# A decoder trunk's last down projection: square sums and products of its tails by halves, residual sums of seven tiles on ScalarE and GpSimd, Newton steps of five tiles on GpSimd

## The chip, the core and the metric

The kernel runs on one core of a Trainium2 chip. The time is device microseconds of one execution. Engines are named as the profile has them: PE (matmul), DVE (vector), ACT (scalar), POOL (GpSimd) and SP, whose queue issues most DMAs.

## The reference

One inference step of a hybrid decoder of two layers, in float32: 1024 prompt tokens and 64 sample tokens, model width 1024, feed-forward width 2816. Layer 0 is a state-space mixer and a convolutional feed-forward block, layer 1 differential attention over a shared cache and another feed-forward block. The change lies in the last lines of layer 1:

```python
def rmsnorm(x, g):
    y = xf * lax.rsqrt(jnp.mean(xf * xf, axis=-1, keepdims=True) + NORM_EPS)
    return (y * g.astype(jnp.float32)).astype(x.dtype)
...
    out = (jax.nn.gelu(gate) * val) @ w_down
...
        f_out, buf = conv_ffn(rmsnorm(x, p['f_pre_g'][i]), conv_buf0[i], p['w_up'][i], p['conv_w'][i],
                              p['conv_b'][i], p['w_down'][i])
        x = x + rmsnorm(f_out, p['f_post_g'][i])
```

So the down projection's output of a token (1024 values) needs the sum of its squares, a reciprocal root, the product with a gain row, and the sum with the residual x; for layer 1 that is the output y.

## The kernel before

Tokens lie on the 128 partitions: eight prompt tiles of 128 tokens (numbered 0 to 7) and one sample tile of 64 (number `NTT` = 8). A tile's result is a 128x1024 accumulator in SBUF, `acc[tt]`.

`ffn_down` works through the 2816 rows of the weight in chunks. In the last layer the last chunk has four blocks of 128 rows and goes by pairs of tiles: first the sample tile, then pairs (0,1), (2,3), (4,5), (6,7) (`LORD`). A pair is one level of a Strassen-Winograd scheme over two tiles and two 512-column halves: seven products (`b11`, `t1`, `t2`, `b21`, `b22`, `t3`, `t4`), each two times three float32 matmuls of 128x512 (each operand is a high and a low part), into PSUM. After each, `add` (L1426 to L1428) has DVE add a PSUM bank to one half of an accumulator: `acc<-mm,acc`, 128x512. Operand sums for the scheme are made by POOL from `gr` (loaded from DRAM scratch `gd`, L1355; sums L1360 to L1363) and split into high and low parts by ACT (L144) and DVE (L145).

`pair` is a generator. The loop over steps runs its seven parts with j = 0 to 6, and at j = 2 does three things: `flush` runs the last part of the pair before, `dn.upto` loads for the next pair, and `finish` calls `done` for the tiles in `ends`. In the last pair of the last layer (`norm` is False) `finish` is not called there; it is called after the loop.

`done` calls `tail_a`: a square sum of the whole tile on ACT (L824, with an accumulator read of 0.19 us), the product with the gain row on DVE (L851), `rstd_from` (L111 on: two small DVE instructions L120 and L123, then three Newton steps of two instructions each, L130 and L134, on one element a partition; with `aside` the steps go to POOL, L126 and L127), the residual sum in one DVE instruction (L854: acc times the root plus x) and the output's DMA on SP's queue (L855). Tile 7 does product, sum and output in two halves. After each tail, `fetch` (L1383) issues the load of the residual x for a tile three or four further on, `xr<-x3d` or `raw<-x3d`.

`part`, used elsewhere in the kernel, is the form of the tail's beginning by a piece: a square sum of a slice, one small DVE instruction (L838, or L835 for a second piece) and the product of the slice (L839). `rstd_from` then takes the partial value as `pre` and uses L122 in place of L120.

The order of the instructions on each engine is fixed when the kernel is built: a scheduler lays the operations out by its own estimates of their times and of what each waits for. On the chip each engine runs its queue in that order.

Of the kernel before, what the change touches and what calls it, by code (L numbers as in the profile page):

```python
# [15 lines left out]
ALU = mybir.AluOpType  # L16
# [5 lines left out]
D = 1024  # L22
# [6 lines left out]
NTT = SEQ // P  # L29
# [44 lines left out]
def trunk_kernel(ctx, tc, I, O):  # L74
    nc = tc.nc
    V = nc.vector
    A = nc.scalar
    PE = nc.tensor
    GP = nc.gpsimd
# [733 lines left out]
    def tokens(tt):  # L813
        return (tt * P, P) if tt < NTT else (SEQ, TS)
# [6 lines left out]
    def square_sum(y, n):  # L821
        junk = slot("junk", dtype=BF16)
        ss = slot("ss")
        A.activation(junk[0:n, 0 : y.shape[1]], y, AF.Square, accum_out=ss[0:n])  # L824
        return ss[0:n]
# [3 lines left out]
    def part(y, tt, post, cs):  # L829

        n = tokens(tt)[1]
        ss = square_sum(y, n)
        if tt in sums:
            p = sums[tt]
            V.scalar_tensor_tensor(p, ss, -0.5 / D, p, op0=ALU.mult, op1=ALU.add)  # L835
        else:
            p = sums[tt] = pools["ph"].tile([P, 1], F32, tag=f"pre{tt}", name=nm("pre"), bufs=1)[0:n]
            V.tensor_scalar(p, ss, -0.5 / D, -0.5 * EPS, op0=ALU.mult, op1=ALU.add)  # L838
        V.tensor_tensor(y, y, post[0:n, cs], ALU.mult)  # L839

    def tail_a(y, tt, post, xsrc, xdst, last=False, rest=slice(0, D), aside=False, xr=None):


        t0, n = tokens(tt)
        if xr is None:
            xr = slot("xr")
            nc.sync.dma_start(xr[0:n], xsrc(tt))
        halves = (slice(512, D), slice(0, 512)) if last else (slice(0, D),)
        ss = square_sum(y[:, rest], n)
        for hs in halves if last else (rest,):  # L850
            V.tensor_tensor(y[:, hs], y[:, hs], post[0:n, hs], ALU.mult)  # L851
        r = rstd_from(pools["ph"], ss, 1, n, "n1", bufs=4, pre=sums.pop(tt, None), aside=aside)
        for hs in halves:
            V.scalar_tensor_tensor(y[:, hs], y[:, hs], r[0:n], xr[0:n, hs], op0=ALU.mult, op1=ALU.add)  # L854
            nc.sync.dma_start(xdst(tt)[:, hs], y[:, hs])  # L855

    def tail_n(y, tt, aside, gain=None):
# [515 lines left out]
    def ffn_down(dn, i, xsrc, xdst, norm):  # L1373
        acc, res = {}, {}
        post = [None]
        nch = len(dn.plan)

        def fetch(j):

            if not norm and j <= NTT:  # L1380
                tt = ORDER[j]
                r = slot("xr") if j % 2 else pools["w"].tile([P, 1024], F32, tag="raw", name=nm("raw"), bufs=2)
                nc.sync.dma_start(r[0 : tokens(tt)[1]], xsrc(tt))  # L1383
                res[tt] = r

        def done(tt):
            n = tokens(tt)[1]
            y = acc[tt][0:n, 0:D]
            if n < P:
                for h in range(2):  # L1390
                    hs = slice(512 * h, 512 * h + 512)
                    u = slot("gr")
                    A.copy(u[0:n], acc[tt][n : 2 * n, hs])
                    V.tensor_tensor(y[:, hs], y[:, hs], u[0:n], ALU.add)
            if norm:
                tail.add(y, tt, post[0], xsrc, xdst)
            else:
                tail_a(y, tt, post[0], xsrc, xdst, tt == NTT - 1, xr=res.pop(tt))
                fetch(ORDER.index(tt) + 4)

        def plain(k, c, tt):
            kind, f0, nf = dn.plan[c]
            n = tokens(tt)[1]
            if c == 0:
                acc[tt] = slot("acc")
            gx, ws = dn.gx.pop(k), dn.ws[c]
            pa = [psum(), psum()]
            for f in range(nf):
                wh, wl = ws[f]
                st, sp = f == 0, f == nf - 1  # L1410
                if n == P:
                    seq = ((gx[:, f, 0:P], wh), (gx[:, f, 0:P], wl), (gx[:, f, P : 2 * P], wh))
                else:
                    seq = ((gx[:, f, 0 : 2 * n], wh), (gx[:, f, 0 : 2 * n], wl))
                for j, (lt, wt) in enumerate(seq):
                    for h in range(2):
                        PE.matmul(pa[h], lt, wt[:, h * 512 : (h + 1) * 512],  # L1417
                                  start=st and j == 0, stop=sp and j == len(seq) - 1)
            for h in range(2):
                a = acc[tt][:, h * 512 : (h + 1) * 512]  # L1420
                if c == 0:
                    A.copy(a, pa[h])
                else:
                    V.tensor_tensor(a, pa[h], a, ALU.add)

        def add(tt, h, ps):  # L1426
            a = acc[tt][:, h * 512 : (h + 1) * 512]
            V.tensor_tensor(a, ps, a, ALU.add)  # L1428

        def sample(k, c):  # L1430
            gx, ws = dn.gx.pop(k), dn.ws[c]

            def prod(ps, o, w, start):
                for e in range(2):
                    for j in range(2):
                        PE.matmul(ps, gx[:, 2 * e + o, 0 : 2 * TS], ws[e, w][j], start=start and e + j == 0,  # L1436
                                  stop=e + j == 2, skip_group_check=True)

            p1, p2 = psum(), psum()
            prod(p1, 0, "b11", True)  # L1440
            add(NTT, 1, p1)
            prod(p2, 0, "t1", True)
            prod(p2, 1, "b22", False)
            add(NTT, 1, p2)
            prod(p1, 1, "b21", False)
            add(NTT, 0, p1)

        def pair(k, c, ta):

            gx, ws = dn.gx.pop(k), dn.ws[c]  # L1450

            def prod(ps, w, start):
                for e in range(2):
                    (ah, al), (wh, wl) = gx[e], ws[e, w]
                    o = dn.AOP[w]
                    mm3(ps, ah[:, o], al[:, o], wh, wl, start and e == 0, e == 1, True)

            p1, p2 = psum(), psum()
            prod(p1, "b11", True)
            add(ta, 0, p1)  # L1460
            yield
            prod(p2, "t1", True)
            add(ta + 1, 1, p2)
            yield
            yield
            prod(p1, "t2", False)
            add(ta, 1, p1)
            yield
            p3 = psum()
            prod(p3, "b21", True)  # L1470
            add(ta, 0, p3)
            yield
            prod(p2, "b22", False)
            add(ta, 1, p2)
            yield
            prod(p1, "t3", False)
            add(ta + 1, 1, p1)
            yield
            prod(p1, "t4", False)
            add(ta + 1, 0, p1)  # L1480
            yield

        rest, ends = [], []

        def flush():

            while rest:
                g, cn = rest.pop()
                next(g)
                dn.load(cn, 1)  # L1490

        def finish():
            while ends:
                done(ends.pop(0))

        for k, (c, tt) in enumerate(dn.steps):
            kind, f0, nf = dn.plan[c]
            if c == nch - 1 and post[0] is None:
                post[0] = row_bcast(I["f_post_g"][i])
                for j in range(4):  # L1500
                    fetch(j)
            if kind == "p":
                dn.upto(k + 2)
                plain(k, c, tt)
                flush()
                if c == 0:
                    dn.load(1, 2)
            elif tt == NTT:
                sample(k, c)
                flush()  # L1510
                dn.upto(k + 1)
                finish()
            else:
                last = tt == 6
                g = pair(k, c, tt)
                for j in range(7):
                    if j == 2:
                        flush()
                        dn.upto(k + 1)
                        if not (norm is False and last):  # L1520
                            finish()
                    next(g)
                    if last and j != 2:
                        dn.load(c + 1, 1)
                if not last:
                    dn.load(c + 1, 1 if norm and c == nch - 2 else (3, 2, 2)[tt // 2])
                rest.append((g, c + 1 if last else nch))
            if c == nch - 1:
                ends += [tt] if kind == "p" or tt == NTT else [tt, tt + 1]
                if kind == "p":  # L1530
                    finish()
        flush()
        finish()
        tail.norm()
# [569 lines left out]
```

## Time and profile before

| | us |
|---|---|
| median of three runs | 2679.99 (2677.94 to 2682.68) |
| the profiled execution | 2684.83 |
| its span, first to last instruction | 2682.9 |
| TensorE clock granted, mean of the span | 0.976 |
| PE, DVE, ACT, POOL busy over the span | 2500.6, 1963.5, 1270.9, 657.3 |
| first residual sum of the stage (sample tile, L854) | from 2638.46 |
| last transfer's issue to the span's end | 2679.02 to 2682.9 |

The profile was taken in an execution of its own, so its span is set against 2684.83 and not against the median. Times in its timeline count from the span's start. The stage that the change touches is the last 60 us. A row of the timeline is start, duration, engine, line, operation, output tile, input tiles, and in brackets the idle time ahead of it with what ended it. DVE's instructions overlap a little: an instruction's duration is some 0.06 to 0.08 us more than the distance to the next start.

### The profile page before, as it was taken

How to read it: one execution, taken by the hardware profiler on the slowest of the kernel's cores; microseconds unless marked ns; L12 is line 12 of the kernel's file. 1: busy time of each engine (PE TensorE's matmuls, PEld its weight loads, DVE VectorE, ACT ScalarE, POOL GpSimd, SP SyncE). 2: the span in 40 equal slices, each digit the busy share in tenths (PEclk: the TensorE clock that was granted, in tenths of full speed). 3: DMA queues.
4: the chain of work that ended last, by engine and by line, in shares of the span. 5: the costliest groups of instructions: out<-in, count | busy, mean ns of one | idle time of the engine just before them, and what ended most of it. 6: DMA issues, size and time to landing. Idle time of an engine off the chain costs nothing.

```text
span 2682.9 us, 39622 instructions
## 1 busy us (share of the span) xinstructions
PE 2500.6 (93%) x14234; PEld 2203.5 (82%) x14234; DVE 1963.5 (73%) x3683; ACT 1270.9 (47%) x2559; POOL 657.3 (24%) x1062
## 2 busy tenths in 40 slices
PE   3778998999999989999999899989799999998997
PEld 2777887999999967778777788877699999996775
DVE  7994358777777789984232688875877777778999
ACT  6763334444444454354322677764544444444432
POOL 3220030111111175501201222113011111137661
PEclk9999998999999999999999899999899999999998
DMA  5443233222222233444646433335322222233334
GB/s 145 99 98 88 85 124 124 65 83 74 74 74 74 89 116 92 127 145 166 204 157 211 104 79 95 97 105 171 115 69 79 74 74 74 74 104 107 94 102 145
DMA packets 265688, 286.77 MB, mean 107 GB/s; under 512 B 42268, under 2 KB 212564, under 8 KB 265492
## 3 DMA queue, kind: packets, MB, share of 16 engines
q1 hardware_dynamic: 261892, 273.55, 33.0%
q0 software_dynamic: 3088, 9.77, 1.7%
q8 instruction: 113, 1.85, 0.3%
q10 hardware_dynamic: 512, 0.92, 0.1%
q14 instruction: 83, 0.68, 0.1%
HBM read 193.58 MB, written 70.93 MB: 99 GB/s over the span
## 4 chain that ended last, share of the span: by engine, by line
PE 58%; DVE 13%; DMA 4%; issue 3%; ACT 3%; POOL 2%; SPq 0%; DVEq 0%; POOLq 0%; ACTq 0%
PE mm L809 17%; PE mm L810 17%; PE mm L811 17%; DVE acc L1428 2%; DMA gr<-gd 1%; DVE xT_lo L145 1%; DVE S L1898 1%; PE mm L1417 1%; ACT S L1902 1%; DVE wst L145 1%; DVE xT_hi L145 1%; DVE acc L854 1%; PE mm L1436 1%; PE tr L870 1%; PE mm L1926 1%
## 5 line engine op out<-in xcount | busy, mean ns | idle before, releaser
L809 PE MATMUL mm<-xT_hi,whi 128*128 128x384 f32 (+1 forms) x1408 | 457.0, 325 | 2.0 <-ACT acc L1146 1.8
L810 PE MATMUL mm<-xT_lo,whi 128*128 128x384 f32 (+1 forms) x1408 | 456.3, 324 | 1.6 <-DVE xT_lo L145 1.6
L811 PE MATMUL mm<-xT_hi,wlo 128*128 128x384 f32 (+1 forms) x1408 | 454.2, 324 | 0.0
L809 PEld LDWEIGHTS mm<-xT_hi,whi 128*128 128x128 f32 x1408 | 265.4, 189 | 3.8 <-ACT acc L1146 2.4
L810 PEld LDWEIGHTS mm<-xT_lo,whi 128*128 128x128 f32 x1408 | 265.7, 189 | 2.4 <-DVE xT_lo L145 2.3
L811 PEld LDWEIGHTS mm<-xT_hi,wlo 128*128 128x128 f32 x1408 | 265.4, 189 | 0.8
L1195 POOL COPY cvo<-acc 128x2 f32<-128x2 f32 x88 | 53.3, 606 | 818.5 <-ACT acc L1178 818.5
L809 PE MATMUL mm<-whi,xT_hi 128*128 128x512 f32 x608 | 243.9, 404 | 4.9 <-ACT whi L792 4.7
L1192 DVE SCALAR_TENSOR_TENSOR acc<-acc,cpar,acc 128x1104 f32<-128x1104 f32 x176 | 240.0, 1385 | 4.7 <-ACT acc L1190 4.6
L810 PE MATMUL mm<-wlo,xT_hi 128*128 128x512 f32 x608 | 241.9, 398 | 0.1
L811 PE MATMUL mm<-whi,xT_lo 128*128 128x512 f32 x608 | 241.7, 399 | 0.0
L144 ACT CAST whi<-raw 128x1024 fp32r<-128x1024 f32 x88 | 92.5, 1051 | 253.5 <-PE mm L811 245.2
L1428 DVE TENSOR_TENSOR acc<-mm,acc 128x512 f32<-128x512 f32 x279 | 184.7, 680 | 9.8 <-PE mm L811 9.3
L145 DVE TENSOR_TENSOR wlo<-raw,whi 128x1024 fp32r<-128x1024 f32 x88 | 107.7, 1224 | 107.0 <-PE mm L810 91.6
L809 PE MATMUL mm<-acc,whi 128*128 128x384 f32 x528 | 179.1, 339 | 0.0
L811 PE MATMUL mm<-acc,wlo 128*128 128x384 f32 x528 | 178.7, 339 | 0.0
L810 PE MATMUL mm<-acc,whi 128*128 128x384 f32 x528 | 178.3, 338 | 0.0
L809 PEld LDWEIGHTS mm<-whi,xT_hi 128*128 128x128 f32 x608 | 115.6, 191 | 36.2 <-ACT whi L792 5.6
L810 PEld LDWEIGHTS mm<-wlo,xT_hi 128*128 128x128 f32 x608 | 114.7, 189 | 27.8 <-DVE wlo L793 0.8
L811 PEld LDWEIGHTS mm<-whi,xT_lo 128*128 128x128 f32 x608 | 114.4, 188 | 27.6 <-issue 0.8
L1190 ACT ACTIVATE acc<-acc,cpar 128x1104 f32<-128x1104 f32 x88 | 114.1, 1311 | 18.1 <-DVE acc L1161 11.9
L145 DVE TENSOR_TENSOR wlo<-xr,whi 128x1024 fp32r<-128x1024 f32 x88 | 107.6, 1223 | 16.7 <-ACT whi L144 8.6
(572 smaller groups left out, 6255.9 us busy)
## 6 DMA issues: line engine op xcount, KB each, us to landing
raw<-in_w_up_dram SPq DMA_DIRECT2D x88, 512.0 KB
gd<-acc SPq DMA_DIRECT2D x44, 552.0 KB
raw<-in_w_down_dram SPq DMA_DIRECT2D x44, 512.0 KB
gr<-gd SPq DMA_DIRECT2D x80, 256.0 KB
raw<-in_glu_w_dram SPq DMA_DIRECT2D x40, 256.0 KB
acc<-in_cache_k_dram SPq DMA_DIRECT2D x16, 512.0 KB
acc<-in_cache_v_dram SPq DMA_DIRECT2D x16, 512.0 KB
xj<-in_x_prompt_dram SPq DMA_DIRECT2D x8, 512.0 KB
```

The costliest lines, as they stand in the source:

```text
L144: A.copy(hi_ap, ps_ap)
L145: V.tensor_tensor(lo_ap, ps_ap, hi_ap.bitcast(F32), ALU.subtract)
L809: PE.matmul(out, lh, rh, start=start, stop=False, **kw)
L810: PE.matmul(out, lh, rl, start=False, stop=False, **kw)
L811: PE.matmul(out, ll, rh, start=False, stop=stop, **kw)
L854: V.scalar_tensor_tensor(y[:, hs], y[:, hs], r[0:n], xr[0:n, hs], op0=ALU.mult, op1=ALU.add)
L870: PE.transpose(ps[:, c * n : (c + 1) * n], y[:, c * P : (c + 1) * P], ident[0:n, 0:n])
L1190: A.activation(hc, hb[:, 2 : 2 + TG], AF.Identity, bias=cp[:, ft, 3:4], scale=cp[:, ft, 2:3])
L1192: V.scalar_tensor_tensor(hc, hb[:, tap : tap + TG], cp[:, ft, tap : tap + 1], hc, op0=ALU.mult, op1=ALU.add)
L1195: GP.tensor_copy(co[:, 0:2], hb[:, SEQ : SEQ + 2])
L1417: PE.matmul(pa[h], lt, wt[:, h * 512 : (h + 1) * 512], start=st and j == 0, stop=sp and j == len(seq) - 1)
L1428: V.tensor_tensor(a, ps, a, ALU.add)
```

## The change

In the last chunk of the last layer:

- Each prompt tile's accumulator has a half that is complete before the other: half (tt mod 2). As soon as that half is complete, `pair` calls `part` on it (`ended`): square sum of 128x512 on ACT, L838, and the product L839 on DVE. `tail_a` later does the other half (`rest`), with the first half's value as `pre`. The sample tile is done whole.
- `done(ta)`, for the pair's first tile, is called within `pair` as soon as its second half is complete. The second tile of the pair is still done by `finish`, which is now called at j = 2 in the last pair too.
- For the tiles in `OFFN` (sample, 0, 1, 2, 3) the Newton steps go to POOL.
- For the tiles in `OFFS` (sample, 0 to 5) the residual sum is done by ACT (product with the root, in place) and POOL (sum with x) in place of one DVE instruction. Tiles 6 and 7 keep the DVE form (now L857).

```diff
--- before.py
+++ after.py
@@ -838,7 +838,7 @@
             V.tensor_scalar(p, ss, -0.5 / D, -0.5 * EPS, op0=ALU.mult, op1=ALU.add)
         V.tensor_tensor(y, y, post[0:n, cs], ALU.mult)
 
-    def tail_a(y, tt, post, xsrc, xdst, last=False, rest=slice(0, D), aside=False, xr=None):
+    def tail_a(y, tt, post, xsrc, xdst, last=False, rest=slice(0, D), aside=False, xr=None, off=False):
 
 
         t0, n = tokens(tt)
@@ -847,11 +847,14 @@
             nc.sync.dma_start(xr[0:n], xsrc(tt))
         halves = (slice(512, D), slice(0, 512)) if last else (slice(0, D),)
         ss = square_sum(y[:, rest], n)
-        for hs in halves if last else (rest,):
-            V.tensor_tensor(y[:, hs], y[:, hs], post[0:n, hs], ALU.mult)
+        V.tensor_tensor(y[:, rest], y[:, rest], post[0:n, rest], ALU.mult)
         r = rstd_from(pools["ph"], ss, 1, n, "n1", bufs=4, pre=sums.pop(tt, None), aside=aside)
         for hs in halves:
-            V.scalar_tensor_tensor(y[:, hs], y[:, hs], r[0:n], xr[0:n, hs], op0=ALU.mult, op1=ALU.add)
+            if off:
+                A.mul(y[:, hs], y[:, hs], r[0:n])
+                GP.tensor_tensor(y[:, hs], y[:, hs], xr[0:n, hs], ALU.add)
+            else:
+                V.scalar_tensor_tensor(y[:, hs], y[:, hs], r[0:n], xr[0:n, hs], op0=ALU.mult, op1=ALU.add)
             nc.sync.dma_start(xdst(tt)[:, hs], y[:, hs])
 
     def tail_n(y, tt, aside, gain=None):
@@ -1395,8 +1398,19 @@
             if norm:
                 tail.add(y, tt, post[0], xsrc, xdst)
             else:
-                tail_a(y, tt, post[0], xsrc, xdst, tt == NTT - 1, xr=res.pop(tt))
+
+                tail_a(y, tt, post[0], xsrc, xdst, tt == NTT - 1, rest=half(tt, 1), xr=res.pop(tt),
+                       aside=tt in OFFN, off=tt in OFFS)
                 fetch(ORDER.index(tt) + 4)
+
+        OFFN, OFFS = (NTT, 0, 1, 2, 3), (NTT, 0, 1, 2, 3, 4, 5)
+
+        def half(tt, j):
+
+            if tt == NTT:
+                return slice(0, D)
+            h = (tt + j) % 2
+            return slice(512 * h, 512 * h + 512)
 
         def plain(k, c, tt):
             kind, f0, nf = dn.plan[c]
@@ -1448,6 +1462,11 @@
         def pair(k, c, ta):
 
             gx, ws = dn.gx.pop(k), dn.ws[c]
+            end = c == nch - 1 and not norm
+
+            def ended(tt):
+                if end:
+                    part(acc[tt][:, half(tt, 0)], tt, post[0], half(tt, 0))
 
             def prod(ps, w, start):
                 for e in range(2):
@@ -1469,12 +1488,16 @@
             p3 = psum()
             prod(p3, "b21", True)
             add(ta, 0, p3)
+            ended(ta)
             yield
             prod(p2, "b22", False)
             add(ta, 1, p2)
+            if end:
+                done(ta)
             yield
             prod(p1, "t3", False)
             add(ta + 1, 1, p1)
+            ended(ta + 1)
             yield
             prod(p1, "t4", False)
             add(ta + 1, 0, p1)
@@ -1517,8 +1540,7 @@
                     if j == 2:
                         flush()
                         dn.upto(k + 1)
-                        if not (norm is False and last):
-                            finish()
+                        finish()
                     next(g)
                     if last and j != 2:
                         dn.load(c + 1, 1)
@@ -1526,7 +1548,7 @@
                     dn.load(c + 1, 1 if norm and c == nch - 2 else (3, 2, 2)[tt // 2])
                 rest.append((g, c + 1 if last else nch))
             if c == nch - 1:
-                ends += [tt] if kind == "p" or tt == NTT else [tt, tt + 1]
+                ends += [tt] if kind == "p" or tt == NTT else [tt, tt + 1] if norm else [tt + 1]
                 if kind == "p":
                     finish()
         flush()
```

Line numbers move: in the changed kernel the product is L850, the residual sum L854 (ACT), L855 (POOL) or L857 (DVE), the output L858, the load of `gr` L1358, the operand sums on POOL L1363 to L1366, the load of x L1386 and `add`'s sum L1442.

Where the instructions stand. On POOL, at the end of its queue, `acc_3983`, `3989`, `3998`, `4002` and `4006` are the accumulators of tiles 1 to 5, `rr_4296` is tile 3's root. In the changed kernel:

```order
L126 TENSOR_SCALAR rs_4295_25463<-rr_4296_25464,rv_4294_25462 128x1
L127 TENSOR_SCALAR rr_4296_25464<-rs_4295_25463,rr_4296_25464 128x1
L126 TENSOR_SCALAR rs_4295_25463<-rr_4296_25464,rv_4294_25462 128x1
L855 TENSOR_TENSOR acc_3983_23328<-acc_3983_23328,raw_4220_25083 128x1024
L127 TENSOR_SCALAR rr_4296_25464<-rs_4295_25463,rr_4296_25464 128x1
L855 TENSOR_TENSOR acc_3989_23356<-acc_3989_23356,xr_4221_25085 128x1024
L855 TENSOR_TENSOR acc_3998_23389<-acc_3998_23389,raw_4244_25213 128x1024
L855 TENSOR_TENSOR acc_4002_23416<-acc_4002_23416,xr_4254_25261 128x1024
L855 TENSOR_TENSOR acc_4006_23441<-acc_4006_23441,raw_4271_25345 128x1024
```

In the kernel before, POOL's queue ends with the operand sums of the last pair (L1360 to L1363); it has no instruction on an accumulator.

On DVE, the queue in the stretch of the last pair of the changed kernel; `acc_4002`, `4006`, `4013`, `4023` are tiles 4, 5, 6, 7, `acc_4217` is the gain row, `mm` are PSUM banks, `rr_4306` is tile 4's root:

```order
L850 TENSOR_TENSOR acc_4002_23416<-acc_4002_23416,acc_4217_25077 128x512
L122 SCALAR_TENSOR_TENSOR rv_4304_25510<-ss_4303_25507,pre_4301_25496 128x1
L838 TENSOR_SCALAR pre_4309_25534<-ss_4308_25532 128x1
L123 TENSOR_SCALAR rr_4306_25512<-rv_4304_25510 128x1
L839 TENSOR_TENSOR acc_4006_23441<-acc_4006_23441,acc_4217_25077 128x512
L130 SCALAR_TENSOR_TENSOR rs_4305_25511<-rr_4306_25512,rv_4304_25510 128x1
L1442 TENSOR_TENSOR acc_4023_23536<-mm_4311_25538,acc_4023_23536 128x512
L1442 TENSOR_TENSOR acc_4013_23490<-mm_4310_25537,acc_4013_23490 128x512
L134 SCALAR_TENSOR_TENSOR rr_4306_25512<-rs_4305_25511,rr_4306_25512 128x1
L1442 TENSOR_TENSOR acc_4006_23441<-mm_4285_25408,acc_4006_23441 128x512
L130 SCALAR_TENSOR_TENSOR rs_4305_25511<-rr_4306_25512,rv_4304_25510 128x1
```

Products, small root steps and PSUM sums (L1442) take turns here. Before, this stretch held whole-tile products (L851) and the residual sums of tiles 1 to 3.

The last PSUM sum of the stage (tile 7) and what DVE had behind it, before:

```order
L1428 TENSOR_TENSOR acc_4023_23536<-mm_4287_25478,acc_4023_23536 128x512
L854 SCALAR_TENSOR_TENSOR acc_3998_23389<-acc_3998_23389,rr_4284_25436,raw_4244_25212 128x1024
L123 TENSOR_SCALAR rr_4304_25577<-rv_4302_25575 128x1
L130 SCALAR_TENSOR_TENSOR rs_4298_25559<-rr_4299_25560,rv_4297_25558 128x1
L854 SCALAR_TENSOR_TENSOR acc_4002_23416<-acc_4002_23416,rr_4294_25543,xr_4259_25311 128x1024
L851 TENSOR_TENSOR acc_4023_23536<-acc_4023_23536,acc_4217_25077 128x512 x2
```

And the end of DVE's queue in the changed kernel, from tile 7's second product on:

```order
L850 TENSOR_TENSOR acc_4023_23536<-acc_4023_23536,acc_4217_25077 128x512
L130 SCALAR_TENSOR_TENSOR rs_4324_25611<-rr_4325_25612,rv_4323_25610 128x1
L122 SCALAR_TENSOR_TENSOR rv_4331_25647<-ss_4330_25644,pre_4328_25633 128x1
L134 SCALAR_TENSOR_TENSOR rr_4325_25612<-rs_4324_25611,rr_4325_25612 128x1
L123 TENSOR_SCALAR rr_4333_25649<-rv_4331_25647 128x1
L857 SCALAR_TENSOR_TENSOR acc_4013_23490<-acc_4013_23490,rr_4325_25612,xr_4281_25393 128x1024
L130 SCALAR_TENSOR_TENSOR rs_4332_25648<-rr_4333_25649,rv_4331_25647 128x1
```

Before, five residual sums of whole tiles and both of tile 7 stood behind the last PSUM sum; now one whole tile's (tile 6) and the two of tile 7 do.

On SP's queue, the last loads of `gr` and the first outputs, before (`acc_3967` is the sample tile, `acc_3977` tile 0):

```order
L1355 DMA gr_4250_25279<-gd_78 128x2x256
L855 DMA out_y_sample_dram<-acc_3967_23270 64x1024
L1383 DMA raw_4244_25212<-x3d_80 128x1024
L1355 DMA gr_4269_25384<-gd_78 128x2x256
L855 DMA out_y_prompt_dram<-acc_3977_23300 128x1024
L1383 DMA xr_4259_25311<-x3d_80 128x1024
L1355 DMA gr_4272_25398<-gd_78 128x2x256
```

And in the changed kernel:

```order
L1358 DMA gr_4260_25299<-gd_78 128x2x256
L1358 DMA gr_4262_25312<-gd_78 128x2x256
L858 DMA out_y_sample_dram<-acc_3967_23270 64x1024
L1386 DMA raw_4244_25213<-x3d_80 128x1024
L1358 DMA gr_4287_25431<-gd_78 128x2x256
L1358 DMA gr_4290_25445<-gd_78 128x2x256
L858 DMA out_y_prompt_dram<-acc_3977_23300 128x1024
```

The sample tile's output stands ahead of the last two loads of `gr` in the changed kernel, and tile 0's output behind both.

## The prediction

> **What bounds the kernel now.** I read the page first, then the end of the span in four windows, then the timeline and the chain of waits there.
>
> ```profile
> span 2682.9 us, 39622 instructions
> PE 2500.6 (93%) x14234; PEld 2203.5 (82%) x14234; DVE 1963.5 (73%) x3683; ACT 1270.9 (47%) x2559; POOL 657.3 (24%) x1062
> ```
>
> Over the span PE is the bound, but the change lies in the last 60 us, and there it is another engine. The windows' columns are PE, PEld, DVE, ACT and POOL busy (instructions), PE clock, DMA share, GB/s:
>
> ```profile
> 2600.00:2620.00 20.00, 18.39 (x80) 14.71 (x79) 18.47 (x33) 6.80 (x15) 11.15 (x18) 1.00 0.26 79
> 2620.00:2640.00 20.00, 20.00 (x88) 16.19 (x87) 19.84 (x44) 7.85 (x16) 6.02 (x8) 1.00 0.33 106
> 2640.00:2660.00 20.00, 17.39 (x71) 13.20 (x70) 19.27 (x46) 6.63 (x14) 3.83 (x8) 0.97 0.38 118
> 2660.00:2683.00 23.00, 6.75 (x24) 4.78 (x22) 18.91 (x58) 3.45 (x6) 0.00 (x0) 0.72 0.63 229
> ```
>
> DVE is busy 58.02 of the 59 us from 2620 to 2679. ACT is a third busy or less, and POOL does nothing after 2660. The timeline shows the last matmul, DVE's last instruction and the last transfers' issue:
>
> ```profile
> 2667.31 0.39 PE L811 MATMUL mm<-xT_hi,xT_lo 128*128 128x512 f32 x1
> 2672.32 7.03 SPq L855 DMA_DIRECT2D out_y_prompt_dram<-acc  x5
> 2677.58 1.42 DVE L854 SCALAR_TENSOR_TENSOR acc<-acc,rr,raw 128x512 f32<-128x512 f32 x2
> ```
>
> DVE works 11.3 us beyond the last matmul (2667.70 to 2679.00), and the span ends 3.9 us after DVE. So at the end a microsecond on DVE is a microsecond of the kernel, as long as the last matmul and the last tile's own chain don't become later than DVE's queue.
>
> **What leaves DVE.** The chain of waits is DVE's queue there, and shows what one instruction holds it (start, us, what):
>
> ```profile
> 2672.30 1.20 DVE acc L851 x2
> 2673.56 0.13 DVE rs L130
> 2673.69 0.07 DVE rr L134
> 2673.76 0.07 DVE rr L123
> ...
> 2674.49 1.20 DVE acc L854
> ```
>
> Seven residual sums at 1.20 leave: 8.4. Fifteen Newton pairs at 0.13 + 0.07 leave: 3.0. What comes: eight first-half sums (L838, priced like L123) at 0.07, 0.6 in all; eight products cut in two, where two halves took 1.20 against 1.14 whole (rows 2672.30 above, 2666.52 below), 0.4 in all. DVE's own work falls by 8.4 + 3.0 − 0.6 − 0.4 = **10.4 us**.
>
> ```profile
> 2666.52 1.14 DVE acc L851
> ```
>
> **What ACT and POOL get.** Groups of the same shapes elsewhere in this kernel; the last two rows give the shortest, median and longest:
>
> ```profile
> L862 ACT ACTIVATE acc<-acc,rr 128x1024 f32<-128x1024 f32 x8 | 8.9, 1145 | 1.9 <-DVE rr L134 1.9
> L1804 POOL TENSOR_TENSOR qwl<-qraw,qwh 128x1024 fp32r<-128x1024 f32 x8 | 19.1, 2389 | 92.7 <-ACT qwh L1803 92.7
> L1870 POOL TENSOR_TENSOR kh<-qraw,kh 128x1024 fp32r<-128x1024 f32 x1 | 3.2, 3200 | 5.6 <-ACT kh L1869 5.6
> L126 POOL TENSOR_SCALAR rs<-rr,rv x60: 333/340/2375, 368.5 to 1877.6; 128x1 f32<-128x1 f32 x48, 64x1 f32<-64x1 f32 x12
> L127 POOL TENSOR_SCALAR rr<-rs,rr x60: 254/264/1237, 369.0 to 1878.0; 128x1 f32<-128x1 f32 x48, 64x1 f32<-64x1 f32 x12
> ```
>
> ACT gets seven products of 1.15, 8.0 us, beside 10 us of work in the last 43: hidden as sums, though they stand ahead of square sums in ACT's queue. POOL gets seven adds of 2.39, **16.7 us** (22.4 at the longest row, 3.20), and 15 Newton pairs of 0.60, 9.1 us. POOL is busy 3.83 us in the 43 from 2640, so as an engine it has room. A reader who stops here forecasts a gain.
>
> **What the adds do to DVE.** The trace has POOL adds beside DVE. The first instruction below is otherwise a 1.22 us one (shortest and median of its seven, 3.43 the longest); the second handles two elements a partition:
>
> ```profile
> L1936 DVE TENSOR_TENSOR oh<-oh,rr x7: 1220/1220/3429, 1550.7 to 1759.5; 128x1024 f32<-128x1024 f32 x7
> ```
>
> ```profile
> 1473.69 2.54 POOL L1804 TENSOR_TENSOR qwl<-qraw,qwh 128x1024 fp32r<-128x1024 f32 x1 [5.32 <-ACT qwh L1803]
> 1473.93 2.32 DVE L132 TENSOR_TENSOR rs<-rr 128x2 f32<-128x2 f32 x1
> ...
> 1759.51 2.37 POOL L1870 TENSOR_TENSOR qx<-qraw,qx 128x1024 fp32r<-128x1024 f32 x1 [4.83 <-ACT qx L1869]
> 1759.54 3.43 DVE L1936 TENSOR_TENSOR oh<-oh,rr 128x1024 f32<-128x1024 f32 x1
> ```
>
> L1936 began with POOL's add and lasted the add (2.37) and then nearly its own 1.22. The tiny L132 ended at 1476.25, 0.02 after POOL's add. So a DVE instruction that reads two operands from SBUF stands still until POOL's instruction is over. It goes the other way too, and one kind of DVE instruction is exempt:
>
> ```profile
> 2629.06 1.29 DVE L851 TENSOR_TENSOR acc<-acc,acc 64x1024 f32<-64x1024 f32 x1
> 2629.35 1.52 POOL L1363 TENSOR_TENSOR gr<-gr,gr 128x128 f32<-128x128 f32 x1
> 2634.32 0.46 POOL L1363 TENSOR_TENSOR gr<-gr,gr 128x128 f32<-128x128 f32 x1
> ```
>
> ```profile
> L1428 DVE TENSOR_TENSOR acc<-mm,acc 128x512 f32<-128x512 f32 x89 | 58.6, 679 | 0.1
> ```
>
> POOL's L1363 lasted 1.52 behind the L851, and 0.46 five microseconds on. L1428, which adds PSUM to SBUF, averages 0.679 over 89 instructions from 2540 on, POOL busy or not: it is not held.
>
> The Trainium skill, "SBUF — State Buffer", section "SBUF: two separate sides", states this as a rule: VectorE and GpSimd share one port pair, an exclusive lock that is held for a whole instruction, whichever starts first; it counts a DVE op with two SBUF inputs among those that need it. These rows agree, 2.32 us for a two-element op among them. By the rule each add of POOL costs DVE up to its whole length; without it the sum would be rival A's.
>
> **The sum.** In the changed order, what stands on DVE next to the seven adds is mostly of the held kind: products (L839, L850), Newton steps (L130, L134), splits (L145); PSUM adds (0.60 apart) come one or two at a time between them. I laid the queues end to end with the durations above. Bounds: nothing held, 0; everything held, 7 × 2.39 = 16.7. What is held:
> - sample's add against a split L145: 1.7; tile 0's against the L839 of tile 2: 2.3
> - tile 1's against the L850 of tile 4: 1.6; tile 2's against the L839 of tile 5: 2.2; tile 3's against tile 4's first L130: 2.2
> - tile 4's against the L850 of tile 6: 2.3; tile 5's against tile 7's Newton steps: 2.2
>
> That is 14.5 of 16.7: each a whole add, less one PSUM add or two small steps that DVE does before it comes to an instruction of the held kind (2.39 − 0.6 to 0.8, or 2.39 − 0.1 to 0.2).
>
> Two terms follow. First, PE waits for PSUM buffers and accumulators behind the held DVE, and PE slows after a thin stretch:
>
> ```profile
> 2655.46:2658.87 3.41, 1.82 (x7) 1.19 (x7) 3.41 (x11) 0.00 (x0) 0.00 (x0) 1.00 0.00 0
> 2658.87:2662.28 3.41, 3.41 (x10) 2.63 (x9) 3.37 (x12) 1.15 (x2) 0.00 (x0) 0.50 0.02 5
> ```
>
> With PE 1.82 of 3.41 us busy, the clock granted in the next 3.41 us was 0.50. One more such stretch costs at most half of it, 1.7; nothing, if DVE's queue covers it. I take 1.5, since PE and DVE alternate there. The Trainium skill, "TensorE: Matmul & The Clock Gate", gives about 3.4 us as the window over which PE's activity is judged; the two rows agree, and the sum uses only them.
>
> Second, the last tile. Before, its square sum on ACT ran while DVE had other tiles' sums to do; now DVE has less to put beside it, and tile 6's and 7's sums (1.20 each) stand behind tile 5's add. Bounds 0 and 2.4 (one add); I take the middle, 1.2.
>
> Sum: −10.4 + 14.5 + 1.5 + 1.2 = **+6.8 us**, about 0.25 %.
>
> Other edits I cost at nothing. The 15 Newton pairs on POOL make tiles 0 to 3 ready later (0.60 against 0.20 a pair, 1.2 a tile); nobody but POOL's adds and the output waits for these, and outputs of 512 KB before the last have room (transfers take 63 % of the end window); with that cover gone, 1.2. Calling the finished tiles earlier moves the sample's output ahead of the last two loads of pre-added activations (gr<-gd) in SP's queue, and tile 0's output behind them. Before, PE idled 2.6 us in 2640 to 2660 (17.39 of 20), part of it for the last such load, which the chain of waits has behind SP's issue of tile 0's output:
>
> ```profile
> 2643.47 0.34 SPq L855
> 2643.86 0.42 SPq L1383
> 2644.39 0.03 SPq L1355
> 2644.45 5.83 DMA gr<-gd
> ```
>
> So this is worth between −1.4 and +1.4; I take 0, because the sample's output now waits for POOL.
>
> The profiled execution took 2684.83 us, 1.93 more than its span and 4.8 above the median of 2679.99. The difference is added to either: 2691.6 for a profile like it, **2686.8** against the median.
>
> **Rivals.**
> - A, the adds hold nothing (faster). It decides if POOL's adds fall beside DVE's PSUM adds and gaps. DVE loses 10.4, but then the last tile's own chain ends the kernel. Its square sum was of a whole tile:
>
> ```profile
> 2669.81 1.06 ACT L824 ACTIVATE gr<-acc 128x1024 bf16<-128x1024 f32 x1 [3.63 <-DVE acc L1428]
> 2670.77 0.19 ACT L824 ACTIVATION_READ_ACCUMULATOR gr<-acc 128x1 f32 x1
> ```
>
> ```profile
> 2676.06 0.21 DVE L130 SCALAR_TENSOR_TENSOR rs<-rr,rv 128x1 f32<-128x1 f32 x1
> 2677.38 0.16 DVE L134 SCALAR_TENSOR_TENSOR rr<-rs,rr 128x1 f32<-128x1 f32 x1
> ```
>
> From the last matmul's end at 2667.70: its add 0.68, a half's square sum 0.53 + 0.19, two small steps 0.3, three Newton pairs of 0.37 as dependent steps, two half sums 1.42: 2671.9 against 2679.0, so −7.1: 2672.9. For it: L1428 is never held. Against: the held rows above; all seven adds read two SBUF tiles.
> - B, half held (no change). If each add starts just as DVE begins two or three PSUM adds, 0.60 × 2.5 = 1.5 of 2.39 is covered, and the held time is 7 × 0.9 = 6.3: −10.4 + 6.3 + 1.5 + 1.2 = −1.4; with three quarters held +4.8. 2678.6 to 2684.8. For it: 58.6 of DVE's some 137 busy us from 2540 on are L1428. Against: five of the seven adds come late, with few L1428 left.
> - C, POOL itself ends the kernel (slower). The last five adds stand back to back; at 3.20 each (the longest row) and each waiting for a 1.2 us DVE instruction in between, they take 5 × 4.4 = 22 us against 5 × 3.6 = 18 at 2.39. It decides when POOL's add of tile 5 ends after DVE's tile 7: +4 on top, 2691.
>
> **How the numbers follow.** Forecast (adds held, +4 to +9) 0.52; B (−2 to +4) 0.26; A 0.14; C 0.08. A difference of 0.2 %, 5.4 us, is about what a measurement of this kernel can tell from no change. Slower by more: C and 0.42 of the forecast's 0.52, 0.50. Same: B and the forecast's lower end, 0.36. Faster: A, 0.14. The range leaves out A and half of C: from B's 2678.5 to 2691.
>
> **What would show it.** Right: DVE rows of L839, L850, L130 at over 2 us beside the POOL adds of L855; the PSUM adds still at 0.68; the last matmul several us later than 2667; POOL's adds stretched where a DVE product started first. Wrong: DVE idle in the last 20 us while those rows have their normal length (A), or adds that begin and end within runs of L1442 (B). An add of 3 us or more is C. If the last matmul is not later though DVE was held, the clock term is wrong.

## The result and the profile after

The changed kernel took 2689.0 us (median of 20 runs, 2682.44 to 2693.76), the kernel before 2681.51 us (20 runs, 2677.35 to 2685.75): a ratio of 1.0029 with a 95% interval of 1.0022 to 1.0035, so by the ratio 7.8 us slower (5.9 to 9.4); the two medians differ by 7.5. The forecast was +6.8; its 2686.8 started from the median of three runs, 2679.99.

The profiled execution of the changed kernel took 2688.97 us, its span 2687.2. Spans of single executions differ by several microseconds in stages that no edit touches, so below each trace is also measured from one fixed instruction: the 600th matmul before the last, 165 us ahead of the end. It starts at 2517.72 before and at 2513.32 after:

```profile
2517.72 0.40 PE L811 MATMUL mm<-xT_hi,xT_lo 128*128 128x512 f32 x1
```

```profile
2513.32 0.40 PE L811 MATMUL mm<-xT_hi,xT_lo 128*128 128x512 f32 x1
```

From there to the span's end are 165.2 us before (2682.9) and 173.9 after (2687.2): **+8.7 us** in this stage. The table of experiments calls this "the stage".

Counted from the same instruction, the last matmul starts at 149.6 before (2667.31) and at 159.7 after (2673.05, row below), so 10.1 us later; DVE's last instruction ends at 161.3 and at 170.9, 9.6 later. The loss thus arises before the last matmul; behind it the changed kernel is 1.4 us shorter. Up to its last instruction DVE was busy 156.35 us before and 162.68 after, and idle 4.9 and 8.2 (columns as before: PE, PEld, DVE, ACT, POOL):

```profile
2517.72:2679.00 161.28, 144.07 (x601) 112.58 (x599) 156.35 (x305) 58.35 (x125) 74.15 (x104) 0.97 0.38 117
2513.32:2684.23 170.91, 146.27 (x601) 114.25 (x599) 162.68 (x284) 68.16 (x148) 105.37 (x142) 0.95 0.36 112
```

The windows at the end of the changed kernel (columns as before):

```profile
2600.00:2620.00 20.00, 20.00 (x88) 16.16 (x87) 18.47 (x33) 7.51 (x16) 7.28 (x13) 1.00 0.30 91
2620.00:2640.00 20.00, 17.74 (x77) 14.07 (x75) 19.16 (x35) 11.07 (x25) 11.64 (x21) 1.00 0.33 101
2640.00:2660.00 20.00, 16.65 (x60) 13.10 (x61) 17.41 (x31) 8.56 (x20) 16.26 (x29) 0.83 0.24 79
2660.00:2687.00 27.00, 7.70 (x26) 5.24 (x24) 22.69 (x51) 6.84 (x13) 11.69 (x5) 0.73 0.52 194
```

From 2640 to 2660 DVE did 31 instructions in 17.41 us, where before it did 46 in 19.27. Part of what counts as busy isn't work: a DVE instruction that is held by POOL counts as busy until it is over. The timeline of the changed kernel shows it; POOL's rows are the seven new adds, DVE's are the ones next to them:

```profile
2632.82 2.83 DVE L145 TENSOR_TENSOR xT_hi<-gr,xT_lo 128x256 fp32r<-128x256 f32 x2
2632.84 2.64 POOL L855 TENSOR_TENSOR acc<-acc,raw 64x1024 f32<-64x1024 f32 x1
2639.05 3.26 DVE L839 TENSOR_TENSOR acc<-acc,acc 128x512 f32<-128x512 f32 x1
2639.42 2.33 POOL L855 TENSOR_TENSOR acc<-acc,xr 128x1024 f32<-128x1024 f32 x1
...
2657.22 2.41 POOL L855 TENSOR_TENSOR acc<-acc,raw 128x1024 f32<-128x1024 f32 x1
2658.01 0.69 DVE L1442 TENSOR_TENSOR acc<-mm,acc 128x512 f32<-128x512 f32 x1 [0.71 <-PE mm L811]
2658.61 1.57 DVE L850 TENSOR_TENSOR acc<-acc,acc 128x512 f32<-128x512 f32 x1
2660.28 2.37 POOL L855 TENSOR_TENSOR acc<-acc,xr 128x1024 f32<-128x1024 f32 x1
2660.36 2.84 DVE L839 TENSOR_TENSOR acc<-acc,acc 128x512 f32<-128x512 f32 x1
2662.60 2.79 POOL L855 TENSOR_TENSOR acc<-acc,raw 128x1024 f32<-128x1024 f32 x1
2663.12 2.29 DVE L130 SCALAR_TENSOR_TENSOR rs<-rr,rv 128x1 f32<-128x1 f32 x1
...
2671.66 2.89 POOL L855 TENSOR_TENSOR acc<-acc,xr 128x1024 f32<-128x1024 f32 x1 [6.27 <-ACT acc L854]
2672.30 2.26 DVE L122 SCALAR_TENSOR_TENSOR rv<-ss,pre 128x1 f32<-128x1 f32 x1
2674.74 0.68 DVE L839 TENSOR_TENSOR acc<-acc,acc 128x512 f32<-128x512 f32 x1
...
2678.26 3.41 POOL L855 TENSOR_TENSOR acc<-acc,raw 128x1024 f32<-128x1024 f32 x1 [3.71 <-ACT acc L854]
2679.39 2.29 DVE L130 SCALAR_TENSOR_TENSOR rs<-rr,rv 128x1 f32<-128x1 f32 x1
```

Each of the seven adds has a DVE row stretched beside it: a half product that takes 0.68 alone (2674.74) takes 3.26 and 2.84, and a step on one element a partition 2.29. Less their usual lengths (the two splits 0.61, a half product 0.68, L130 0.21, L122 0.15) the stretches are 2.2, 2.6, 0.9, 2.2, 2.1, 2.1 and 2.1: 14.2 us. The adds lose too: 2.79, 2.89 and 3.41 in place of 2.39, where a DVE instruction had begun first. The PSUM sums stay at their length: the one at 2658.01 lies wholly within tile 1's add and took 0.69, and all of them from 2540 on:

```profile
L1442 DVE TENSOR_TENSOR acc<-mm,acc 128x512 f32<-128x512 f32 x86 | 56.8, 679 | 4.6 <-PE mm L811 4.3
```

What follows from a held DVE is seen on PE. Behind tile 0's add and the 3.26 us product, PE waited 5.28 us for the next PSUM sum, and the 3.41 us stretch behind that ran at half clock. The last matmul started at 2673.05:

```profile
2643.02 0.80 PE L809 MATMUL mm<-wst,xT_lo 128*128 128x512 f32 x1 [5.28 <-DVE acc L1442]
2673.05 0.39 PE L811 MATMUL mm<-xT_hi,xT_lo 128*128 128x512 f32 x1
```

```profile
2639.60:2643.02 3.42, 0.00 (x0) 0.00 (x0) 3.42 (x4) 0.51 (x1) 2.69 (x3) 0.80 0.29 81
2643.02:2646.43 3.41, 3.41 (x8) 2.74 (x9) 3.19 (x8) 1.74 (x5) 1.88 (x5) 0.50 0.08 10
```

### The profile page after: what moved, and what is told of

The parts are those of the page before. It is cut to its first block, busy times and chain, and to the rows that moved or that the text cites. A ratio compares the mean times of both kernels' runs of the same rounds, so it can differ in the third digit from the quotient of the medians.

```text
span 2687.2 us, 39661 instructions
## 1 busy us (share of the span) xinstructions
PE 2498.4 (93%) x14234; PEld 2202.8 (82%) x14234; DVE 1972.7 (73%) x3661; ACT 1281.5 (48%) x2582; POOL 681.8 (25%) x1099
## 4 chain that ended last, share of the span: by engine, by line
PE 58%; DVE 14%; DMA 3%; issue 3%; ACT 3%; POOL 2%; SPq 0%; DVEq 0%; ACTq 0%; POOLq 0%
PE mm L809 17%; PE mm L810 17%; PE mm L811 17%; DVE acc L1442 2%; DVE S L1920 1%; DMA gr<-gd 1%; DVE xT_lo L145 1%; PE mm L1431 1%; DVE xT_hi L145 1%; ACT S L1924 1%; DVE wst L145 1%; PE mm L1948 1%; PE mm L1450 1%; DVE S L1934 1%; PE tr L873 1%
## 5 line engine op out<-in xcount | busy, mean ns | idle before, releaser
L1442 DVE TENSOR_TENSOR acc<-mm,acc 128x512 f32<-128x512 f32 x279 | 184.4, 679 | 12.2 <-PE mm L811 11.7
L1181 ACT COPY acc<-mm 128x256 f32<-128x256 f32 x88 | 32.4, 368 | 184.2 <-PE mm L811 184.2
```

What stands on the lines that cost most here:

```text
L1181: A.copy(hb[:, 2 + n0 : 2 + SEQ], ps[:, 0:wp])
```

## The experiments

The theory, H: a POOL instruction that reads SBUF holds every DVE instruction with two SBUF operands until it is over, and the seven adds do that at the kernel's end. The rivals: the loss comes from the other parts of the change (order, loads behind outputs, Newton steps on POOL), or from the longer chain ACT, POOL, output. All runs, with the ratio to the kernel before, what it makes in microseconds, and the stage from one trace each, against 165.2:

| run | ratio (95%) | us | stage, us |
|---|---|---|---|
| the change | 1.0029 (1.0022 to 1.0035) | +7.8 | +8.7 |
| e1 no sums on POOL | 1.0002 (0.9993 to 1.0010) | +0.5 | -0.2 |
| e2 halves only | 0.9999 (0.9988 to 1.0009) | -0.3 | -1.3 |
| e3 sums on POOL, Newton on DVE | 1.0011 (1.0001 to 1.0021) | +2.9 | +5.0 |
| e4 sums on ACT and DVE | 1.0003 (0.9995 to 1.0012) | +0.8 | +0.7 |
| e5 before, spare POOL adds | 1.0050 (1.0031 to 1.0069) | +13.4 | +11.8 |
| e6 before, spare POOL memsets | 0.9991 (0.9980 to 1.0003) | -2.4 | -0.3 |
| e7 POOL adds in four pieces | 1.0017 (1.0006 to 1.0028) | +4.6 | +4.8 |
| e8 POOL Newton: sample, tile 0 | 1.0032 (1.0021 to 1.0043) | +8.6 | +9.7 |
| e9 POOL Newton: tiles 1, 2, 3 | 1.0002 (0.9993 to 1.0011) | +0.5 | +3.2 |
| e10 POOL sums: tiles 1 to 5 | 1.0004 (0.9995 to 1.0013) | +1.1 | +5.5 |
| e11 POOL sums: sample, tile 0 | 1.0005 (0.9996 to 1.0014) | +1.3 | +3.7 |
| e12 halves, POOL Newton: tiles 2, 3 | 1.0002 (0.9993 to 1.0011) | +0.5 | -0.3 |

The stage comes from one execution a kernel and is the weaker number; where the two columns differ, the interval decides.

### Which part of the change costs: e1 to e4

e1 puts the sums back on DVE, e2 the Newton steps too, e3 only the Newton steps:

```diff
-        OFFN, OFFS = (NTT, 0, 1, 2, 3), (NTT, 0, 1, 2, 3, 4, 5)
+        OFFN, OFFS = (NTT, 0, 1, 2, 3), ()                        # e1
+        OFFN, OFFS = (), ()                                       # e2
+        OFFN, OFFS = (), (NTT, 0, 1, 2, 3, 4, 5)                  # e3
```

> The changed kernel with the seven residual sums back on DVE as one instruction each (halves, and Newton steps of five tiles on POOL, stay). Theory H, POOL's seven adds hold DVE: without them nothing is held but by the 0.3 us steps; DVE's own work is 3.0 less and 1.0 more than in the kernel before, so about 2 us faster than before (-4 to 0), the last matmul within 2 us of before's. Rival O, the loss is in the rest (order of the queues, loads behind other outputs, late Newton steps): still 4 us or more slower than before.

> Halves alone: residual sums and all Newton steps on DVE. H: DVE has 1.0 us more than before and nothing new is held: -1 to +2 against before. O: 4 us or more slower than before.

> The changed kernel with all Newton steps on DVE (halves and POOL's seven sums stay). H: seven holds as in the changed kernel, and 3.0 us more on DVE: +8 to +11 against before. If the Newton steps on POOL are what costs: at most +4.

e4 keeps ACT's product and moves only the add:

```diff
-                GP.tensor_tensor(y[:, hs], y[:, hs], xr[0:n, hs], ALU.add)
+                V.tensor_tensor(y[:, hs], y[:, hs], xr[0:n, hs], ALU.add)
```

> The changed kernel with the seven adds on DVE in place of POOL; ACT still multiplies by the root first. H: DVE pays 1.14 an add in place of 1.20 for the one-instruction form, no holds: -4 to 0 against before, as with the sums wholly on DVE. If ACT's seven products in front of square sums are the cost: +4 or more.

Without POOL's sums the loss is gone: e1 +0.5 (-1.9 to +2.7), e2 -0.3 (-3.2 to +2.4). e4 makes the same seven adds behind the same seven ACT products, on DVE, and takes +0.8 (-1.3 to +3.2): it is neither the earlier calls nor ACT's products, but where the add runs. From e2 to e3 only the sums move to ACT and POOL. e3's own stretched rows hold 14.6 us, and 14.6 less 8.4 of DVE's work makes +6.2, which is what the two traces differ by in the stage. The runs say less: e3 took +2.9 (+0.3 to +5.6), some 3 more than e2. So the holds are there, but not all of their time need show in the kernel's.

Two expectations missed. e1 was to gain 2 us by the Newton steps that leave DVE and gained nothing that its interval shows, and e3, with all Newton steps on DVE, was to take +8 to +11 and be slower than the change; it was faster than the change by some 5. e4's +0.8 lies above its -4 to 0, but its interval takes them in in part. The waits of DVE in e1, from 2610 on (microseconds, times, longest), show the first:

```profile
DVE acc L857 <- POOL rr L127: 2.7, 3, 1.3
```

The root comes later from POOL, and DVE's queue stands behind the residual sum that waits for it: 2.7 us, nearly the 3.0 saved. Up to its last instruction DVE was busy 2.3 us less than in e2 and idle 3.4 more.

### The hold alone: e5 and e6

Both are the kernel before with a POOL instruction more behind each of seven residual sums; it writes over x, which nobody reads again, and the output stays the same.

```diff
             V.scalar_tensor_tensor(y[:, hs], y[:, hs], r[0:n], xr[0:n, hs], op0=ALU.mult, op1=ALU.add)
             nc.sync.dma_start(xdst(tt)[:, hs], y[:, hs])
+            if more:
+                GP.tensor_tensor(xr[0:n], y, xr[0:n], ALU.add)    # e5
+                GP.memset(xr[0:n], 0.0)                           # e6
```

> The kernel before, with one more POOL instruction behind each of the seven residual sums of the sample and tiles 0 to 5: it adds the finished tile and x into x's buffer, which nobody reads again (the output is the same). It is the same form as the change's add, but nothing waits for its result except the next load into that buffer. H (a POOL add of two SBUF tiles holds DVE's two-operand instructions for its whole length): seven holds of up to 2.4, the last ones partly behind DVE's end: +7 to +14 against before, with DVE rows of 1 to 2.4 us beside each add. If what costs in the change is its chain from ACT to POOL to the output: 0 to +2, since there is no such chain here.

> As the one with the spare add, but the spare POOL instruction sets x's buffer to zero: it writes as much, waits for the same, and reads nothing. If a hold needs a POOL instruction that reads SBUF: 0 to +2 against before and no stretched DVE rows. If any POOL instruction on SBUF holds DVE: DVE rows stretched to the length of the memset, and 7 times it in time, less what DVE's PSUM sums cover.

The adds, whose result nobody uses, cost 13.4 us (8.3 to 18.5). The memsets cost nothing that shows (-2.4, -5.4 to +0.8). In e5's trace six of the seven adds stretch a DVE row, by 12.9 us in all, and the stage is 11.8 longer. Five of these rows come after the last matmul (2660.14), where DVE's queue sets the end. In the change six of the seven begin before the last matmul. The Newton step L130 on DVE, shortest, median and longest in ns, in the changed kernel, in e5 and in e6 (there from 2655 on, while four of the memsets ran):

```profile
L130 DVE SCALAR_TENSOR_TENSOR rs<-rr,rv x12: 204/214/2295, 2663.1 to 2682.4; 128x1 f32<-128x1 f32 x12
```

```profile
L130 DVE SCALAR_TENSOR_TENSOR rs<-rr,rv x27: 200/208/2381, 2627.0 to 2680.4; 128x1 f32<-128x1 f32 x24, 64x1 f32<-64x1 f32 x3
```

```profile
L130 DVE SCALAR_TENSOR_TENSOR rs<-rr,rv x17: 202/205/207, 2655.6 to 2671.6; 128x1 f32<-128x1 f32 x17
```

In e6 a residual sum from 2665.06 lasted its usual 1.27 although a memset ran beside it from 2665.00:

```profile
2665.00 0.95 POOL L858 MEMSET xr<- 128x1024 f32 x1 [4.56 <-DVE acc L855]
```

```profile
2665.06 1.27 DVE L855 SCALAR_TENSOR_TENSOR acc<-acc,rr,raw 128x1024 f32<-128x1024 f32 x1
```

So it isn't POOL's writing nor its being busy that holds DVE. The Trainium skill, "SBUF — State Buffer", section "SBUF: two separate sides", says of a DVE op with two SBUF inputs that it contends only against a GpSimd op that reads SBUF; the pair of runs agrees (+13.4 and -2.4).

### How long a hold lasts: e7

```diff
-                GP.tensor_tensor(y[:, hs], y[:, hs], xr[0:n, hs], ALU.add)
+                for q in range(4):
+                    qs = slice(256 * q, 256 * q + 256)
+                    GP.tensor_tensor(y[:, qs], y[:, qs], xr[0:n, qs], ALU.add)
```

> The changed kernel with each of POOL's seven adds cut into four of 128x256. H (the hold lasts one instruction): no DVE instruction is held longer than one quarter, about 0.7, and DVE comes in between: +2 to +7 against before, less than the changed kernel by 2 or more. If DVE and POOL shared bandwidth instead, the cut changes nothing: +7 to +9, and POOL's adds take four times their fixed cost more.

```profile
L130 DVE SCALAR_TENSOR_TENSOR rs<-rr,rv x12: 204/358/766, 2664.0 to 2680.6; 128x1 f32<-128x1 f32 x12
```

No L130 was held longer than about a quarter add: 0.77 in place of 2.30. There DVE came in between the pieces. They hold more often (the median rose from 214 to 358 ns), and the time is +4.6 (1.6 to 7.5): less than the change's +7.8 by the medians, but the two intervals overlap.

But the expectation that no DVE instruction is held longer than one piece missed. Tile 0's four pieces stood back to back, and one product was held through all of them; in e3 (the second view) a small step was held through two whole adds and three operand sums behind them:

```profile
2643.04 3.79 DVE L839 TENSOR_TENSOR acc<-acc,acc 128x512 f32<-128x512 f32 x1
2643.47 2.78 POOL L857 TENSOR_TENSOR acc<-acc,xr 128x256 f32<-128x256 f32 x4
```

```profile
2636.03 2.41 POOL L855 TENSOR_TENSOR acc<-acc,raw 64x1024 f32<-64x1024 f32 x1 [4.09 <-ACT acc L854]
2636.08 5.93 DVE L122 SCALAR_TENSOR_TENSOR rv<-ss,pre 128x1 f32<-128x1 f32 x1
2638.41 2.36 POOL L855 TENSOR_TENSOR acc<-acc,xr 128x1024 f32<-128x1024 f32 x1
```

So a hold can last through several POOL instructions that follow each other directly. When DVE comes in between and when not, no run here shows.

### Why Newton steps on POOL cost beside the sums: e8 and e9

```diff
-        OFFN, OFFS = (NTT, 0, 1, 2, 3), (NTT, 0, 1, 2, 3, 4, 5)
+        OFFN, OFFS = (NTT, 0), (NTT, 0, 1, 2, 3, 4, 5)            # e8
+        OFFN, OFFS = (1, 2, 3), (NTT, 0, 1, 2, 3, 4, 5)           # e9
```

> The changed kernel with Newton steps on POOL only for the sample and tile 0; those of tiles 1, 2 and 3, which in POOL's queue stand between the last pair's operand sums, go back to DVE. Theory N1 (they cost by standing among the operand sums and by POOL's own late adds): as with all Newton steps on DVE, +3 to +6 against before. N2 (the first two tiles' steps cost, by when the sample's and tile 0's adds then fall): as the changed kernel, +7 to +9.

> The changed kernel with the Newton steps of the sample and tile 0 back on DVE and those of tiles 1, 2 and 3 on POOL: the other half of the run with two tiles' steps on POOL. N2 (the first two tiles' steps cost): as with all steps on DVE, +3 to +6 against before. N1 (the last three tiles' steps cost): +7 to +9. If either half alone costs the same, the costs don't add: +7 to +9 too.

N2 has the right tiles: with the steps of the sample and tile 0 on POOL +8.6 (5.6 to 11.5), as the change; with the other three's instead +0.5 (-1.9 to +2.9). Its price for e9, +3 to +6, missed. What differs is POOL's order. In the changed kernel the sample's add ran at 2632.84, and the operand sums for the pair (4,5) behind it; in e9 they ran first. Counted from the fixed matmul (2517.99 in e9), the operand sums began at 122.1 in the change and at 115.0 in e9, the add at 119.5 and at 123.4:

```profile
2632.84 2.64 POOL L855 TENSOR_TENSOR acc<-acc,raw 64x1024 f32<-64x1024 f32 x1
2635.46 0.51 POOL L1363 TENSOR_TENSOR gr<-gr 128x128 f32<-128x128 f32 x1
```

```profile
2632.94 0.47 POOL L1363 TENSOR_TENSOR gr<-gr 128x128 f32<-128x128 f32 x1 [16.98 <-DMA gr<-gd]
...
2641.39 3.13 POOL L855 TENSOR_TENSOR acc<-acc,raw 64x1024 f32<-64x1024 f32 x1 [4.09 <-ACT acc L854]
```

In sum, PE waited from 2600 on for a PSUM sum on DVE 11.3 us in the changed kernel, 7.3 in e9, and 8.0 in e8, which is as slow as the change:

```profile
PE mm L809 <- DVE acc L1442: 11.3, 4, 5.3
```

```profile
PE mm L809 <- DVE acc L1442: 7.3, 3, 4.1
```

```profile
PE mm L809 <- DVE acc L1442: 8.0, 4, 5.3
```

So the length of PE's wait does not by itself give the loss. How much of it is the late operand sums and how much the hold at that place wasn't separated.

Counted by holds less work, e9 comes out: its stretched rows hold 12.4, and DVE does 8.4 and 1.8 (nine Newton pairs) less, which makes +2.2, within its interval (its stage is +3.2). The same count for the change makes 14.2 − 8.4 − 3.0 = +2.8, where 7.8 were measured. The other 5 come with the early Newton steps on POOL, by a way that these runs do not settle.

### Which sums: e10 and e11, and a version put together: e12

```diff
-        OFFN, OFFS = (NTT, 0, 1, 2, 3), (NTT, 0, 1, 2, 3, 4, 5)
+        OFFN, OFFS = (NTT, 0, 1, 2, 3), (1, 2, 3, 4, 5)           # e10
+        OFFN, OFFS = (NTT, 0, 1, 2, 3), (NTT, 0)                  # e11
+        OFFN, OFFS = (2, 3), ()                                   # e12
```

> The changed kernel with the sums of the sample and tile 0 back on DVE, so POOL has the adds of tiles 1 to 5 alone. H by its holds: 4.8 of held time less, 2.4 of DVE's work more; if the early holds also keep PE waiting (5.3 us of PE idle behind tile 0's add in the changed kernel), up to 5 less on top: +1 to +5 against before. If all adds cost alike: the changed kernel's +8 less 2 sevenths of it, +5.5 or more.

> The opposite: POOL has the adds of the sample and tile 0 alone, the others are back on DVE. H by its holds: +4.8 of held time, -2.4 of DVE's work against the run without POOL sums, which was as fast as before: +2 to +3; with PE kept waiting on top +4 to +6. If all adds cost alike: 2 sevenths of the changed kernel's +8, about +2.3.

> A version put together from what the runs left standing: halves, all residual sums on DVE in one instruction, and on POOL only the Newton steps of tiles 2 and 3, whose residual sums come last in DVE's queue, so that DVE should not wait for the root as it did for the sample, tile 0 and tile 1 in the run without POOL's sums. DVE's own work 1.2 us less than with halves alone, which was as fast as before: -3 to 0 against before, likely too little to tell from no change. If POOL's steps cost more than they save here too: 0 to +2.

e10 took +1.1 (-1.3 to +3.5) and e11 +1.3 (-1.1 to +3.8). The all-alike price of 5.5 for e10 lies outside its interval, so the two early adds cost more than two sevenths when the late ones are there too; e11's interval takes in both of its smaller prices and settles nothing. The traces' stages (+5.5 and +3.7) are above the medians for both. Neither group alone makes the change's 7.8, and the two don't add up to it within their medians, which stays unexplained. e12 is as fast as the kernel before; no version here beats it.

## Why the prediction came out

**The bound.** Right behind the last matmul: e5 shows that time DVE loses there is time of the kernel. Before the last matmul DVE and PE alternate, and DVE's idle time counts too. Of the 9.6 us by which DVE's queue ended later, 6.3 are busy time (forecast: −10.4 + 14.5 = +4.1) and 3.3 are idle time; behind DVE's end the kernel was 0.9 shorter.

**The holds, 14.5 us.** Right in mechanism, sum and nearly all places: 14.2 in the trace. Predicted and seen, add by add: 1.7 and 2.2, 2.3 and 2.6, 1.6 and 0.9, 2.2 and 2.2, 2.2 and 2.1, 2.3 and 2.1, 2.2 and 2.1. Six of the seven were on the instruction named; tile 4's add caught the small L122 behind tile 6's product, not the product. In the changed kernel L850 never passed 2 us, as I had said it would. Whether held time is always paid in full is open: the recorded expectation for e3, made by this sum, was +8 to +11, and +2.9 was measured.

**DVE's own work, −10.4.** It fell by 7.9 (busy +6.3 less 14.2 held). The sums and the Newton steps did leave; what came back beyond the forecast is in part short stretches beside POOL's small instructions, such as 1.18 us for an L850 at 2637.55 that otherwise takes 0.68. The cut into halves was charged 1.0: DVE is busy 1.1 us longer in e2 than before, too little for e2's time to tell. The step that failed is "fifteen Newton pairs leave: 3.0" with the price of nothing for POOL's later roots. Alone they save nothing that shows, since DVE waits 2.7 for them (e1); beside POOL's sums they cost about 5 (the change against e3, 1.0029 and 1.0011). I had named POOL's adds and the outputs as all that waits for POOL's roots. In the changed kernel the residual sums of these tiles aren't on DVE, so e1's wait isn't there; what was missed is that 0.60 us a pair in POOL's queue also moves what stands behind it, the operand sums that PE needs. That it is the early steps which cost is shown (e8 and e9); that they cost by these operand sums is argued.

**The clock, +1.5, and the last tile, +1.2.** Half clock came back, in 2643.02 to 2646.43 first. No run prices either term alone. Together they were put at 2.7; what stands against them in the trace is DVE's idle time, up by 3.3 (the row of L1442 above has 4.3 us of waits for PE, L1428's before had 0.1 of waits in all). Against the trace's +8.7 the forecast had DVE's work 2.5 too low and the idle time 0.6 too low, the holds 0.3 too high, and it had nothing for the 0.9 at the end. Errors of opposite sign met: that the total of +6.8 came within 1 of the runs' +7.8 is partly luck, as the miss of the same sum at e3 shows.

**Rivals.** A (nothing held) is out by the seven rows and by e5 against e6. B (half held): 14.2 of 16.7 were held. C (POOL ends the kernel): by the sign that I had named, an add of 3 us or more, POOL's last add at 3.41 speaks for it, but the sign was ill chosen: the add ended at 2681.67 and DVE's last instruction at 2684.23.

**Two sizes.** The "some 137" busy us of DVE from 2540 on in rival B are 134.6. The bounds of 1.4 for the order of the loads stand on no row that was shown, and no run prices that order alone.

## What to carry to other kernels

Before moving an elementwise operation from DVE to POOL, count not POOL's idle time but what DVE has to do beside it: if DVE is full with instructions that read two SBUF operands, the operation can cost DVE POOL's length (2.4 us) in place of its own (1.2). How much of that the kernel pays differed here: nearly all of it in e5, less in e3. Here sums from PSUM and POOL memsets were free of this. Shorter POOL instructions shortened most holds, but not where they followed each other directly. A small step handed to another engine saves little if the queue that it left waits for its result.

## What the runs showed of the hardware

A DVE instruction on a single element a partition was held for 2.1 us as fully as one on 512, and in e3 for 5.8 us through several POOL instructions in a row. A POOL memset of 128x1024 takes 0.95 us and held nothing in e6, an add of the same size 2.33 to 2.41 when it isn't held itself.
